# A seam between two phases laid out anew: one residual instruction, one square, h by pairs of feature tiles, weight splits behind them

## The chip, the core and the metric

The kernel runs on one core of one Trainium2 chip. The metric is the device time of one launch in microseconds. The core's engines are TensorE (PE, with the weight loads shown apart as PEld), VectorE (DVE), ScalarE (ACT), GpSimd (POOL) and SyncE (SP, which only issues DMAs here). Each runs its own instructions in order, and waits for the others by semaphores.

## What is computed

Two layers of a transformer block with three parts: half a feed-forward (ffn a), a token mixer, half a feed-forward (ffn b). They run on 256 latent tokens `x` and 256 context tokens `ctx`, 1024 features each, in float32:

```python
def _rmsnorm(x, g):
    return x * lax.rsqrt(jnp.mean(x * x, axis=-1, keepdims=True) + EPS) * g

def _half_ffn(x, mod, g_pre, g_post, wg, wu, wd):
    shift, scale, gate = mod
    h = _rmsnorm(x, g_pre) * (1 + scale) + shift
    y = (jax.nn.silu(h @ wg) * (h @ wu)) @ wd
    return x + 0.5 * gate * _rmsnorm(y, g_post)

# mixer: the same frame around m @ w_out, where m is the gated sum of
# a gated linear attention, a Fourier mix and a latent attention over w_in's outputs
# for each layer: ffn a on x and ctx, mixer on both, ffn b on both;
# the last layer's mixer output and ffn b are needed for x alone
```

So between two parts each token row is finished (`x + gate * rmsnorm(y)`), normed again, scaled and shifted by feature, and fed to the next part's first matrix products.

## The kernel before

**Layout.** The 512 tokens (context, then latent) are four *token tiles* of 128 rows: `x` is one SBUF tile [128, 4, 1024] with tokens on partitions. The input of each part, `h`, stands the other way, features on partitions: eight feature tiles [128, 512 tokens]. Every float32 product is made of three matmuls: each operand is split into a hi part (rounded to fp32r) and a lo part (the rest), and hi x hi, lo x hi and hi x lo are summed in PSUM (`acc`, L479 to L481; `mul`, L530 to L532).

**Phases.** There are six: ffn a, mixer, ffn b of each layer. A phase ends in `down`, which multiplies by `wd` (tile name d) or `wout` (o) with tokens on PSUM's partitions, in two column halves of 512. In the second half the last k-tiles, six in an ffn and eight in a mixer, are *held*: `seam` runs them token tile by token tile, so that tile 0 is finished while TensorE still works on tiles 1 to 3. That makes 18 or 24 matmuls a token tile.

**The seam.** In it TensorE, DVE, ACT and POOL keep the order in which the code is written (`manual_schedule`); outside of it a scheduler orders them. For each token tile: `evac` squares and sums the PSUM on ACT (sink<-d, L536) and multiplies it by the gate's row on DVE (dy, L537); `mean_eps` adds the two half sums and EPS on DVE (nv, L450); `root` is a power of -0.5 on POOL (nr, L455); `residual` adds to x in two halves of 512 on DVE (L465), each followed by a square and sum on ACT (sink<-x, L469); then another `mean_eps` and `root`, and `normed_x` makes n on DVE (L474). TensorE transposes n, eight times 128x128, into four PSUM banks pt, each of which holds two feature tiles of 256 tokens (L431). `pre_tile` scales and shifts each feature tile: ACT writes hi straight from PSUM (L440); for even tiles DVE computes the same value unrounded, pnt, from the same bank (L442) and subtracts hi (L443); for odd tiles ACT writes pnt (L445) and POOL subtracts (L446).

Tokens 0 to 255 (n0, n1) are the first half; the transposes of n0 stand after tile 2's held matmuls, those of n1 at two thirds of tile 3's, and their `pre_tile` calls are strewn between tile 3's steps. The second half (n2, n3) is a closure, `late`.

**The next phase** starts with `dense_pair`: three blocks in a mixer (zx, zk, zk; 144 matmuls of 256 columns) or four in an ffn (pg, pu, pg, pu; 192), first for tokens 0 to 255, then for 256 to 511. It calls `late` after the fifth of eight k-steps of the first half. In a mixer the result zx is copied by ACT (zxs, L657), and a chain over DVE, ACT and TensorE follows that ends in the decays; zq are the projections beside it.

**Weights** come as raw tiles of 512 KB through SP's DMA queue into four buffers. `Stream.pump` issues loads as buffers come free, and splits the weights (ACT CAST, L144; DVE subtraction, L145) 8 or 9 half-units ahead of their use. It is called whenever the next half-unit of weights is taken, so within `dense_pair` too.

**The seams** are counted in the text: 0 (ffn a to mixer, layer 0), 1 (mixer to ffn b), 2 (ffn b to ffn a of layer 1), 3 (ffn a to mixer) and 4 (mixer to ffn b, layer 1). Seams 0 to 3 have all four token tiles. Seam 4 has tiles 2 and 3 alone, without an early half, and so has the end, where the rows of x go out instead (four DMAs of 256 KB, L467).

## Time and profile before

| | us |
|---|---|
| median of 3 runs (lowest, highest) | 2222.96 (2221.34, 2223.61) |
| the profiled execution | 2223.26 |
| its span, first to last instruction | 2221.4 |
| TensorE busy | 2123.8 (96%) |
| DVE busy | 1323.6 (60%) |
| ACT busy | 880.2 (40%) |
| POOL busy | 198.5 (9%) |

The mean granted clock of TensorE is 0.986 of full speed. How to read it: an engine's busy share is an average over stages that have different limits. What a change in one stage is worth is read from that stage: where TensorE stood idle in it, for how long, and who released it. The views used below are the windows (busy time of each engine in a stretch), the timeline (instructions in order of time, with the idle time ahead of one in brackets and what ended it), the waits (who waited for whom) and the page's groups. Columns such as 128x512 are partitions by elements. Matmuls overlap, so one that is listed with 0.39 us may follow another after 0.23: paces are read from starts.

### The profile page before, as it was taken

What the parts mean: (1) busy time and instruction counts of PE and PEld (TensorE: products, weight loads), DVE (VectorE), ACT (ScalarE), POOL (GpSimd) and SP (SyncE); (2) the same over time, 40 slices, a digit from 0 to 9 for tenths busy, and PEclk for the clock granted to TensorE, in tenths of its full rate; (3) what the DMA queues carried; (4) which work ended last, traced back from release to release, by engine and by line L of the source; (5) the groups of instructions that cost most, each with busy time, mean ns of one, the idle gap of its engine ahead of it and who ended that gap; (6) DMA issues with size and microseconds to landing.
All of it is one profiled execution on the core that took longest, in us unless ns stands there. A gap on an engine that the chain in (4) does not pass through costs nothing.

```text
span 2221.4 us, 33022 instructions
## 1 busy us (share of the span) xinstructions
PE 2123.8 (96%) x12928; PEld 1791.3 (81%) x12928; DVE 1323.6 (60%) x2554; ACT 880.2 (40%) x1747; POOL 198.5 (9%) x220
## 2 busy tenths in 40 slices
PE   6999999899999999999999989999998999998998
PEld 5788888677777788888888868888887788997997
DVE  4877677567566634478776545333334677765554
ACT  4332223644344523443233344232225545545443
POOL 1000000134120100100000010000001232100000
PEclk9999999999999999999999999999999999998999
DMA  8555476131111223256557615232431323453553
GB/s 306 191 190 198 162 242 213 48 105 40 55 48 58 91 81 128 72 165 203 192 188 267 215 55 172 81 114 76 134 113 39 114 65 96 154 193 131 177 192 123
DMA packets 88436, 304.52 MB, mean 137 GB/s; under 512 B 10520, under 2 KB 13848, under 8 KB 88280
## 3 DMA queue, kind: packets, MB, share of 16 engines
q1 hardware_dynamic: 86328, 296.88, 39.9%
q10 hardware_dynamic: 1952, 5.53, 0.7%
q8 instruction: 101, 1.65, 0.3%
q14 instruction: 55, 0.45, 0.1%
HBM read 301.23 MB, written 1.15 MB: 136 GB/s over the span
## 4 chain that ended last, share of the span: by engine, by line
PE 80%; DVE 6%; ACT 5%; DMA 3%; issue 3%; POOL 2%; ACTq 0%; SPq 0%; POOLq 0%; DVEq 0%
PE d L531 6%; PE d L532 6%; PE d L530 6%; PE pu L481 6%; PE pg L481 6%; PE pu L480 6%; PE pu L479 6%; PE pg L479 5%; PE pg L480 5%; PE ga L481 3%; PE ga L479 3%; PE ga L480 3%; DMA raw<-wmod 2%; PE br L479 1%; PE br L481 1%
## 5 line engine op out<-in xcount | busy, mean ns | idle before, releaser
L145 DVE TENSOR_TENSOR w<-raw,w 128x512 fp32r<-128x512 f32 (+2 forms) x824 | 532.8, 691 | 155.1 <-ACT w L144 152.3
L144 ACT CAST w<-raw 128x512 fp32r<-128x512 f32 (+2 forms) x824 | 460.4, 612 | 298.5 <-DMA raw<-wd 82.2
L303 DVE SCALAR_TENSOR_TENSOR raw<-raw,cbc 128x1024 f32<-128x1024 f32 x128 | 156.5, 1223 | 36.0 <-DMA raw<-wmod 33.7
L303 DVE SCALAR_TENSOR_TENSOR junk<-raw,cbc 128x1024 f32<-128x1024 f32 x96 | 117.2, 1221 | 82.9 <-DMA raw<-wmod 82.8
L610 DVE TENSOR_TENSOR sg<-sg,pu 128x512 f32<-128x512 f32 (+1 forms) x88 | 54.3, 617 | 150.9 <-PE pu L481 136.9
L455 POOL TENSOR_TENSOR nr<-nv,cst 128x1 f32<-128x1 f32 x38 | 21.0, 552 | 1370.5 <-DVE nv L450 1370.5
L609 ACT ACTIVATE sg<-pg 128x512 f32<-128x512 f32 (+1 forms) x88 | 47.4, 540 | 78.5 <-PE pg L481 78.2
L481 PE MATMUL pg<-h10l,w 128*128 128x512 f32 (+1 forms) x192 | 72.0, 376 | 5.6 <-DVE h10l L443 4.2
L479 PE MATMUL ga<-h01h,w 128*128 128x512 f32 x192 | 76.0, 396 | 0.0
L481 PE MATMUL ga<-h01l,w 128*128 128x512 f32 x192 | 75.6, 394 | 0.0
L479 PE MATMUL pg<-h02h,w 128*128 128x512 f32 (+1 forms) x192 | 72.2, 376 | 3.3 <-ACT h02h L440 3.3
L481 PE MATMUL pg<-h02l,w 128*128 128x512 f32 (+1 forms) x192 | 72.5, 378 | 2.7 <-DVE h02l L443 1.5
L480 PE MATMUL ga<-h01h,w 128*128 128x512 f32 x192 | 74.9, 390 | 0.0
L537 DVE TENSOR_TENSOR dy<-d,gr 128x512 f32<-128x512 f32 x28 | 19.1, 690 | 93.0 <-ACT sink L536 92.7
L817 DVE SCALAR_TENSOR_TENSOR tg<-tg,br 128x512 f32<-128x512 f32 (+1 forms) x48 | 26.4, 551 | 77.6 <-PE br L481 68.5
L479 PE MATMUL pg<-h10h,w 128*128 128x512 f32 (+1 forms) x192 | 71.6, 373 | 1.1 <-ACT h10h L440 1.0
L479 PE MATMUL pu<-h10h,w 128*128 128x512 f32 (+1 forms) x192 | 71.5, 372 | 1.0 <-ACT w L144 1.0
L479 PE MATMUL pg<-h00h,w 128*128 128x512 f32 x176 | 69.0, 392 | 3.4 <-ACT h00h L440 3.4
L481 PE MATMUL pu<-h02l,w 128*128 128x512 f32 (+1 forms) x192 | 72.0, 375 | 0.0
L480 PE MATMUL pu<-h02h,w 128*128 128x512 f32 (+1 forms) x192 | 71.9, 375 | 0.0
L480 PE MATMUL pg<-h02h,w 128*128 128x512 f32 (+1 forms) x192 | 71.9, 374 | 0.0
L479 PE MATMUL pu<-h02h,w 128*128 128x512 f32 (+1 forms) x192 | 71.8, 374 | 0.0
(518 smaller groups left out, 5933.4 us busy)
## 6 DMA issues: line engine op xcount, KB each, us to landing
raw<-wgu SPq DMA_DIRECT2D x170, 512.0 KB, 4.3
raw<-wmod SPq DMA_DIRECT2D x128, 512.0 KB, 4.3
raw<-win SPq DMA_DIRECT2D x92, 512.0 KB, 3.4
raw<-wd SPq DMA_DIRECT2D x88, 512.0 KB, 4.2
raw<-wm SPq DMA_DIRECT2D x16, 512.0 KB, 7.8
raw<-wbr SPq DMA_DIRECT2D x16, 512.0 KB, 3.5
raw<-wout SPq DMA_DIRECT2D x16, 512.0 KB, 4.1
gr<-rows SPq DMA_DIRECT2D x10, 512.0 KB, 6.5
```

The costliest lines, as they stand in the source:

```text
L144: nc.scalar.copy(hi, w)
L145: nc.vector.tensor_tensor(lo, w, hi.bitcast(F32), ALU.subtract)
L303: nc.vector.scalar_tensor_tensor(w if r else self.junk, w, 1.0, self.cbc[r], ALU.mult, ALU.mult, accum_out=m[:, t, r:r + 1])
L479: nc.tensor.matmul(ps, lhsT=hi, rhs=rhi, start=first, stop=False)
L480: nc.tensor.matmul(ps, lhsT=lo, rhs=rhi, start=False, stop=False)
L481: nc.tensor.matmul(ps, lhsT=hi, rhs=rlo, start=False, stop=last)
L530: nc.tensor.matmul(ps, lhsT=hi, rhs=w[0], start=kt == 0, stop=False)
L531: nc.tensor.matmul(ps, lhsT=hi, rhs=w[1], start=False, stop=False)
L532: nc.tensor.matmul(ps, lhsT=lo, rhs=w[0], start=False, stop=kt == n - 1)
L609: nc.scalar.activation(sg[:, t0:512], pg[:, t0:512], AF.Silu)
L610: nc.vector.tensor_tensor(sg[:, t0:512], sg[:, t0:512], pu[:, t0:512], ALU.mult)
L817: nc.vector.scalar_tensor_tensor(x, x, 1.0, ps[:, t0:512], ALU.add, ALU.mult)
```

## The change

- `x` and `sink` get a 1025th column, which POOL sets once to (1024 x EPS)^0.5. The square of x over 1025 columns, scaled by 1/1024, then sums to mean + EPS, so that DVE's `mean_eps` for x goes.
- The residual is one DVE instruction of 1024 columns, the square one ACT instruction of 1025 (`squares`), with the root right behind it.
- The transposes of n0 stand in the middle of tile 2's held matmuls, those of n1 in the middle of tile 3's.
- `pre_tile` in the seams becomes `pre_pair`, for two feature tiles at a time: ACT writes both unrounded from the bank (pnt), DVE rounds them to hi in one cast of 2x256 columns and subtracts in another instruction. POOL and DVE no longer make pnt or lo from the bank; POOL keeps the roots alone. The h tiles, which hold two feature tiles each, have names by pair now (h010 is pair 0 of h01).
- `late` comes one k-step later, and within `dense_pair` the stream is `lazy`: it doesn't split weights ahead until `late` has been issued.
- `late` takes the transposes of n2 and n3 by turns, feature tile by feature tile. (The start of the program, which makes the first h, uses the same function for its transposes.)
- The output's rows go out in two DMAs of 512 KB.

```diff
@@ class Stream
+        self.lazy = False
@@ next
-            self.pump()
+            if not self.lazy or self.s not in self.parts:
+                self.pump()
@@ setup
-        self.x = c.tile([128, 4, D], F32, name="x")
-        self.sink = c.tile([128, D], F32, name="sink")
+        self.x = c.tile([128, 4, D + 1], F32, name="x")
+        self.sink = c.tile([128, D + 1], F32, name="sink")
+        nc.gpsimd.memset(self.x[:, :, D:D + 1], (D * EPS) ** 0.5)
...
+    def turned(self, out, ns):
+        for t in range(NT):
+            for j, n in ns:
+                self.nc.tensor.transpose(out[t // 2][:, t % 2, 128 * j:128 * j + 128], n[:, 128 * t:128 * t + 128], self.ident)
+        return out
+    def pre_pair(self, l, which, hf, u, bank):
+        nc = self.nc
+        sl = slice(256 * hf, 256 * hf + 256)
+        A, B = (self.modv[l][3 * which + a] for a in (1, 0))
+        tmp = self.s("pnt", (2, 256))
+        for w in range(2):
+            t = 2 * u + w
+            nc.scalar.activation(tmp[:, w, :], bank[:, w, :], AF.Identity, bias=B[:, t, hf:hf + 1], scale=A[:, t, hf:hf + 1])
+        def parts():
+            hi, lo = self.h2[0][u][:, :, sl], self.h2[1][u][:, :, sl]
+            nc.vector.tensor_copy(hi, tmp)
+            nc.vector.tensor_tensor(lo, tmp, hi.bitcast(F32), ALU.subtract)
+        return parts
...
-    def residual(self, j, r, out):
...
+    def residual(self, j, r):
+        xj = self.x[:, j, 0:D]
+        self.nc.vector.scalar_tensor_tensor(xj, self.y[j], r, xj, ALU.mult, ALU.add)
+    def squares(self, j):
+        sx = self.v("sx", 1)
+        self.nc.scalar.activation(self.sink, self.x[:, j, :], AF.Square, scale=D ** -0.5, accum_out=sx)
+        return self.root(sx)
@@ dense_pair
+        self.W.lazy = True
...
-                if hf == 0 and kt == NT - 4:
+                if hf == 0 and kt == NT - 3:
                     self.late()
+                    self.W.lazy = False
+                    self.W.pump()
@@ seam
         for j in tiles:
             for i, (kt, w) in enumerate(held):
-                if turned and j == last and i == 2 * len(held) // 3:
-                    self.turn_tile(turned, 1, ns[1])
+                if ahead and j >= last - 1 and i == len(held) // 2:
+                    t = j - last + 1
+                    self.turned(pts, [(t, ns[t])])
                 mul(ps[j], kt, w, j)
-            if turned and j == last:
-                half(0, turned, range(2))
+            if ahead and j == last:
+                pair()
+                parts[0]()
+            if nxt and j > first:
+                rx[j - 1] = self.squares(j - 1)
+            if ahead and j == last:
+                pair()
             evac(ps[j], j, 1)
-            if nxt and j > tiles[0]:
-                close(j - 1)
             r = self.root(self.mean_eps(ss[j][:, 0:1], ss[j][:, 1:2]))
-            if turned and j == last:
-                half(0, turned, range(2, 4))
-            sx[j] = self.residual(j, r, nxt is None)
-            if turned and j == last - 1:
-                self.turn_tile(turned, 0, ns[0])
+            if ahead and j == last:
+                parts[1]()
+                pair()
+            if nxt and j > first:
+                close(j - 1)
+            self.residual(j, r)
+            if not nxt:
+                self.nc.sync.dma_start(self.io["out"][j - 2], self.x[:, j, 0:D])
         if nxt:
-            if turned:
-                half(0, turned, range(4, 6))
+            if ahead:
+                parts[2]()
+                pair()
+            rx[last] = self.squares(last)
+            if ahead:
+                parts[3]()
             close(last)
-            if turned:
-                half(0, turned, range(6, NT))
-            self.late = lambda: half(1, self.turned([ns[2], ns[3]]))
+            def late():
+                for u, bank in enumerate(self.turned(self.banks(), [(0, ns[2]), (1, ns[3])])):
+                    self.pre_pair(*nxt, 1, u, bank)()
+            self.late = late
```

DVE in seam 0, from tile 0's residual to tile 1's; dy_2395 and dy_2396 are tiles 0 and 1 before, n_3231 is n0. Before:

```order
397 L465 SCALAR_TENSOR_TENSOR x<-dy_2395,nr,x 128x512 x2
398 L537 TENSOR_TENSOR dy_2396<-d,gr_2441 128x512
399 L450 SCALAR_TENSOR_TENSOR nv<-sx 128x1
400 L474 TENSOR_SCALAR n_3231<-x,nr 128x1024
401 L450 SCALAR_TENSOR_TENSOR nv<-ss_2400 128x1
402 L465 SCALAR_TENSOR_TENSOR x<-dy_2396,nr,x 128x512 x2
```

and now, with dy_2396 as tile 0 and n_3232 as n0:

```order
397 L482 SCALAR_TENSOR_TENSOR x<-dy_2396,nr,x 128x1024
398 L557 TENSOR_TENSOR dy_2397<-d,gr_2442 128x512
399 L472 SCALAR_TENSOR_TENSOR nv<-ss_2401 128x1
400 L491 TENSOR_SCALAR n_3232<-x,nr 128x1024
401 L482 SCALAR_TENSOR_TENSOR x<-dy_2397,nr,x 128x1024
```

Each tile has one row less: the small sum of the squares of x is gone. The instruction of n stands behind the next tile's evacuation and sum in both.

ACT in seam 0, at the second half: the last two of eight weight casts in a row (w) and the late h tiles behind them (h01h from PSUM, pnt unrounded). Before:

```order
253 L144 CAST w_3402<-raw_3375 128x512
254 L144 CAST w_3406<-raw_3375 128x512
255 L440 ACTIVATE h01h_3164<-pt,m_3_1214,m_4_1537 128x256
256 L445 ACTIVATE pnt<-pt,m_3_1214,m_4_1537 128x256
257 L440 ACTIVATE h01h_3165<-pt,m_3_1214,m_4_1537 128x256
258 L144 CAST w_3411<-raw_3389 128x512
259 L440 ACTIVATE h01h_3166<-pt,m_3_1214,m_4_1537 128x256
260 L440 ACTIVATE h01h_3165<-pt,m_3_1214,m_4_1537 128x256
261 L445 ACTIVATE pnt<-pt,m_3_1214,m_4_1537 128x256
```

and now, from tile 3's square (sink<-x) to the first two of nine casts:

```order
238 L486 ACTIVATE sink,sx<-x 128x1025
239 L684 DMA tabq<-tabq 128x1024
240 L447 ACTIVATE pnt<-pt,m_3_1215,m_4_1538 128x256 x8
241 L147 CAST w_3447<-raw_3439 128x512
242 L147 CAST w_3450<-raw_3439 128x512
```

Before, all but one of the second half's twelve instructions stood behind the eight casts, and a ninth cast among them. Now all eight of the second half stand ahead of the casts.

TensorE in seam 0, around the end of tile 2 and the start of tile 3 (a16 to a20 are the held k-tiles in turn). Before:

```order
1586 L531 MATMUL d<-w_3129,a20h_2310 128x512
1587 L532 MATMUL d<-w_3129,a20l_2311 128x512
1588 L431 MATMUL pt<-cst,n_3231 128x128 x8
1589 L530 MATMUL d<-w_3046,a16h_1982 128x512
1590 L531 MATMUL d<-w_3046,a16h_1982 128x512
1591 L532 MATMUL d<-w_3046,a16l_1983 128x512
```

and now, in the middle of tile 2:

```order
1600 L551 MATMUL d<-w_3089,a18h_2143 128x512
1601 L552 MATMUL d<-w_3089,a18l_2144 128x512
1602 L436 MATMUL pt<-cst,n_3232 128x128 x8
1603 L550 MATMUL d<-w_3092,a18h_2143 128x512
1604 L551 MATMUL d<-w_3092,a18h_2143 128x512
1605 L552 MATMUL d<-w_3092,a18l_2144 128x512
```

The transposes of n0 moved by nine matmuls towards the front.

## Rows read from the trace of the kernel before

**Rows 1.** Page part 4, the chain that ended last: share of the span by engine.

```profile
PE 80%; DVE 6%; ACT 5%; DMA 3%; issue 3%; POOL 2%; ACTq 0%; SPq 0%; POOLq 0%; DVEq 0%
```

**Rows 2.** Windows, five seams: stretch; length; busy PE, PEld, DVE, ACT, POOL (count); clock; DMA.

```profile
387.14:432.86 45.72, 37.71 (x232) 32.41 (x230) 25.80 (x50) 25.20 (x58) 11.01 (x16) 0.96 0.19 58
913.20:966.50 53.30, 47.24 (x297) 42.67 (x296) 24.20 (x48) 27.34 (x59) 10.72 (x16) 0.94 0.22 77
1291.64:1343.90 52.26, 42.60 (x279) 37.07 (x279) 30.89 (x59) 27.26 (x60) 11.18 (x16) 1.00 0.31 103
1669.00:1713.40 44.40, 37.16 (x238) 31.70 (x236) 24.65 (x48) 24.15 (x56) 10.94 (x16) 1.00 0.14 48
2005.00:2045.00 40.00, 31.39 (x193) 29.15 (x192) 21.58 (x40) 20.69 (x45) 5.18 (x8) 0.83 0.39 131
```

**Rows 3.** Timeline, TensorE, seam 0: start, us, work, [idle before <- releaser].

```profile
386.98 0.39 PE L530 MATMUL d<-w,a16h 128*128 128x512 f32 x1
...
395.15 1.03 PE L431 MATMUL pt<-cst,n 128*128 128x128 f32 x8
395.94 0.48 PE L530 MATMUL d<-w,a16h 128*128 128x512 f32 x1
...
400.50 1.09 PE L431 MATMUL pt<-cst,n 128*128 128x128 f32 x8 [1.58 <-DVE n L474]
...
422.40 0.38 PE L479 MATMUL zx<-h01h,w 128*128 128x256 f32 x1 [1.63 <-ACT h01h L440]
...
432.14 0.28 PE L480 MATMUL zk<-h01h,w 128*128 128x256 f32 x1
...
432.62 0.28 PE L481 MATMUL zk<-h01l,w 128*128 128x256 f32 x1
```

**Rows 4.** Waits of TensorE: waiter <- releaser, us in total, times, longest.

```profile
PE pt L431 <- DVE n L474: 11.5, 7, 3.1
PE zq L479 <- ACT kq L669: 9.6, 2, 4.9
...
PE pg L479 <- ACT h02h L440: 3.3, 1, 3.3
```

**Rows 5.** Timeline, seam 0: ACT, then DVE, then POOL.

```profile
404.54 0.56 ACT L440 ACTIVATE h01h<-pt,m,m 128x256 fp32r<-128x256 f32 x1 [0.61 <-DVE pnt L442]
...
417.62 4.26 ACT L144 CAST w<-raw 128x512 fp32r<-128x512 f32 x8
...
409.31 1.41 DVE L465 SCALAR_TENSOR_TENSOR x<-dy,nr,x 128x512 f32<-128x512 f32 x2
...
410.07 1.24 POOL L446 TENSOR_TENSOR h01l<-pnt,h01h 128x256 fp32r<-128x256 f32 x1 [0.90 <-ACT pnt L445]
```

**Rows 6.** Page part 5: weight subtraction, 1024-column multiply, root; busy and mean ns.

```profile
L145 DVE TENSOR_TENSOR w<-raw,w 128x512 fp32r<-128x512 f32 (+2 forms) x824 | 532.8, 691 | 155.1 <-ACT w L144 152.3
...
L303 DVE SCALAR_TENSOR_TENSOR raw<-raw,cbc 128x1024 f32<-128x1024 f32 x128 | 156.5, 1223 | 36.0 <-DMA raw<-wmod 33.7
...
L455 POOL TENSOR_TENSOR nr<-nv,cst 128x1 f32<-128x1 f32 x38 | 21.0, 552 | 1370.5 <-DVE nv L450 1370.5
```

**Rows 7.** One line or tile: ns min/median/max. Square, n and POOL's lo part.

```profile
L361 ACT ACTIVATE sink<-x x2: 1039/1048/1057, 5.4 to 8.7; 128x1024 f32<-128x1024 f32 x2
...
L474 DVE TENSOR_SCALAR n<-x,nr x4: 752/753/755, 393.7 to 415.0; 128x1024 f32<-128x1024 f32 x4
...
L446 POOL TENSOR_TENSOR h01l<-pnt,h01h x8: 728/736/1237, 405.6 to 427.8; 128x256 fp32r<-128x256 f32 x8
```

**Rows 8.** Timeline, TensorE, seam 4.

```profile
2020.25 1.97 PE L431 MATMUL pt<-cst,n 128*128 128x128 f32 x8 [2.67 <-DVE n L474]
...
2034.97 0.44 PE L479 MATMUL pu<-h12h,w 128*128 128x256 f32 x1 [2.89 <-ACT sg L609]
```

**Rows 9.** Page part 6, DMA issues: size and median us to landing.

```profile
raw<-win SPq DMA_DIRECT2D x92, 512.0 KB, 3.4
```

**Rows 10.** Line 467, the output's four DMAs of 256 KB.

```profile
DMA to landing us min/median/max: 2.0/2.0/2.0
```

More of the change, by code (lines that the diff above doesn't have):

```diff
@@ L419, in new_h, with banks @@
     def new_h(self, name):
[L420 to L431 removed]
+        self.h2 = [[self.c([2, 512], f"{name}{j}{w}", F32R) for j in range(NT // 2)] for w in "hl"]
+        self.hi, self.lo = ([h[t // 2][:, t % 2, :] for t in range(NT)] for h in self.h2)
+    def banks(self):
+        return [self.aux("pt", (2, 256)) for _ in range(4)]
+    def turned(self, out, ns):
+        for t in range(NT):
+            for j, n in ns:
+                self.nc.tensor.transpose(out[t // 2][:, t % 2, 128 * j:128 * j + 128], n[:, 128 * t:128 * t + 128], self.ident)
+        return out
+    def pre_pair(self, l, which, hf, u, bank):
[11 more added lines that the diff above has]
+        return parts
     def pre_tile(self, l, which, hf, t, n):
@@ L456, in root @@
         return r
-    def residual(self, j, r, out):
-        nc = self.nc
-        sx = self.v("sx", 2)
-        for h in range(2):
-            sl = slice(512 * h, 512 * h + 512)
-            xj = self.x[:, j, sl]
-            nc.vector.scalar_tensor_tensor(xj, self.y[j][:, sl], r, xj, ALU.mult, ALU.add)
-            if out:
-                nc.sync.dma_start(self.io["out"][j - 2][:, sl], xj)
-            else:
-                nc.scalar.activation(self.sink[:, sl], xj, AF.Square, scale=D ** -0.5, accum_out=sx[:, h:h + 1])
-        return sx
+    def residual(self, j, r):
+        xj = self.x[:, j, 0:D]
+        self.nc.vector.scalar_tensor_tensor(xj, self.y[j], r, xj, ALU.mult, ALU.add)
[3 more added lines that the diff above has]
+        return self.root(sx)
     def normed_x(self, j, r):
         n = self.c([D], f"n{j}")
-        self.nc.vector.tensor_scalar(n, self.x[:, j, :], r, None, ALU.mult)
+        self.nc.vector.tensor_scalar(n, self.x[:, j, 0:D], r, None, ALU.mult)
         return n
@@ L563, in seam @@
     def seam(self, tiles, held, ps, mul, evac, ss, nxt):
-        full, last = len(tiles) == 4, tiles[-1]
-        ns, sx = {}, {}
-        turned = [self.aux("pt", (2, 256)) for _ in range(4)] if full and nxt else None
-        def half(hf, banks, ts=range(NT)):
-            for t in ts:
-                self.pre_tile(*nxt, hf, t, banks[t // 2][:, t % 2, :])
+        full, first, last = len(tiles) == 4, tiles[0], tiles[-1]
+        ns, rx = {}, {}
+        ahead = full and nxt
+        pts = self.banks() if ahead else None
@@ L575, in close, with pair @@
+        parts = []
+        def pair():
+            u = len(parts)
+            parts.append(self.pre_pair(*nxt, 0, u, pts[u]))
         def close(j):
-            ns[j] = self.normed_x(j, self.root(self.mean_eps(sx[j][:, 0:1], sx[j][:, 1:2])))
+            ns[j] = self.normed_x(j, rx[j])
         for j in tiles:
             for i, (kt, w) in enumerate(held):
-                if turned and j == last and i == 2 * len(held) // 3:
-                    self.turn_tile(turned, 1, ns[1])
+                if ahead and j >= last - 1 and i == len(held) // 2:
+                    t = j - last + 1
+                    self.turned(pts, [(t, ns[t])])
```

23 lines of the change are left out of this document (8 added, 15 removed).

## The prediction

> **What bounds the kernel now.** I read the page's chain first: TensorE carries 80% of the chain that ended last [rows 1], so time is won only where TensorE stands still or runs slowly. Next I listed TensorE's idle time in order of time. It is bunched in the four full "seams", where one phase hands over to the next: three tiles of held matmuls, 32 transposes, then the first projections in two halves. Each has a row in [rows 2], from the end of tile 0's last held matmul to the last matmul of the projections: 45.72, 53.30, 52.26 and 44.40 us for seams 0 to 3.
>
> What would these stretches take if TensorE never waited? [Rows 3] has the paces: the 36 matmuls of tiles 1 and 2 go from 386.98 to 395.15, so 0.227 each and 4.08 us a tile; eight transposes take 0.79 (395.15 to 395.94); a 256-column matmul takes 0.12 (four in 0.48, 432.14 to 432.62). Seams 0 and 3 are three tiles (12.2), 32 transposes (3.2) and 144 projection matmuls (17.3): 32.7. Seam 2 has 192 matmuls: 38.4. Seam 1 has 24 matmuls a tile (5.45) and 192: 42.5. So 13.0, 10.8, 13.9 and 11.7 us, **49.4 in all, are waiting, or a slow pace after a wait**. That is what the change can win there.
>
> Of what the waits consist is seen in seam 0. TensorE stands 1.58 before the transposes of n1, whose DVE instruction isn't done, and 1.63 before an h tile of the second half (400.50 and 422.40) [rows 3]; over the run the transposes wait 11.5 us for n [rows 4]. The h tiles are late for two reasons [rows 5]: ACT's h waits 0.61 for DVE's pnt, which reads the same PSUM bank, in turn and not beside it; and at 417.62 eight weight casts, 4.26 us, stand on ACT ahead of nearly all of the second half's h tiles.
>
> **The change part by part.** I walk through seam 0 in us after 387.14, with hops of 0.04 to 0.08 between engines.
>
> *Residual and squares.* Two halves take 1.41 on DVE [rows 5]; one 128x1024 instruction of the same kind 1.22 [rows 6], saving 0.2. One Square of 128x1024 takes 1.05 [rows 7], and 0.1 more to its sum; but it can't start until the whole residual is done, where the first half's square ran beside the second half's residual. Dropping the small DVE sum (EPS now comes in as a column) saves 0.2. So the chain per tile is about as long as before: tile 0's residual 2.18 to 3.40, square to 4.65, root (0.55 on POOL [rows 6]) to 5.25. On DVE the next tile's evacuation and sum stand ahead; n0 (0.75 [rows 7]) ends at 6.8.
>
> *Transposes moved.* n0 now stands in the middle of tile 2, at 6.1: wait 0.75. n1 is ready at 11.95 where TensorE wants it at 11.8: wait 0.25. Before, the second waited 1.58. Tile 3 ends at 14.9.
>
> *Pairs instead of tiles.* ACT alone now reads the bank (two instructions of 0.56 [rows 5]), DVE makes the hi part with a new 128x512 cast, and the lo part by a subtraction, 0.69 at most, what the weight's subtraction of that size takes [rows 6]. The cast is not in the trace. Its bounds: half of n's 0.75 [rows 7], thus 0.38, and the two-input subtraction's 0.69. I take the middle, 0.55: n has one input in SBUF as the cast has, but another output type. The walk was made with 0.45; the 0.1 is added below. Pair 0 is complete at 14.75, before tile 3 ends; pairs 1 and 2 cost waits of 0.3 and 0.2; pair 3 (22) is in time. POOL's lo parts, of which one took 1.24 beside a DVE residual [rows 5], are gone.
>
> *Splits behind.* The late transposes follow n3 (22.5) and the eight late ACT instructions run at once, so the second half starts at 25.8 without a wait, where before it waited 1.63. The nine weight casts end at about 31.6, 3 us earlier in time than before's eight, and are covered by the second half's matmuls to 34.4. Without that cover they would hold the copy of zx, and with it the decay chain that ends in zq's wait of 4.8 us in each mixer [rows 4], which remains; for that I add 0 to 1, taken 0.5, a mixer.
>
> Waits left: 1.5, and 0.8 for slow first matmuls behind them: seam 0 takes 35.0 instead of 45.7, **-10.7**; seam 3, the same program, **-9.4**. In seam 1 the tiles are longer, so no transposes wait, and of the 3.3 us that the second half stood there for an h tile [rows 4] I keep 0.9: a table load and two Silus still come ahead of late pair work, the casts no longer. With 0.7 for slow firsts 44.1, **-9.2**. In seam 2 weights are still cast ahead of and between the late pairs: the 1.5 of seam 0, then 0.5, 1.7 and 0.8, and 0.7 for slow firsts, 43.6, **-8.7**.
>
> *Seam 4* works with two tiles and has no second half. Its last transposes stood 2.67 for n, and a later block 2.89 for ACT's sg [rows 8], at a granted clock of 0.83 [rows 2], so partly at the lower of the two levels. The h tiles come some 5 us earlier by pairs, but now the transposes of n2 stand between those of n3, so they can't go early: **-3** (-1.5 to -4.5).
>
> *Ends.* The output goes in 512 KB pieces: the last 256 KB landed in 2.0 [rows 10], a 512 KB load of the quick kind takes 3.4 [rows 9]; less 0.2 for the shorter residual: **+0.6** (0.3 to 1.2, since the first piece no longer goes out ahead). Setting the EPS column (one POOL instruction at the start) and the longer rows of x cost nothing: the loads of x hide them; uncovered, 0.5.
>
> Sum: -10.7 -9.2 -8.7 -9.4 -3 +0.6 = -40.4; +1.0 for the zx chain, +1.6 for the cast, 0.1 for each of four on the path of four seams: **-37.8**. From the profiled execution's 2223.26 (span 2221.4, 1.9 around it; 0.3 above the median of the runs) that is **2185.5**.
>
> One row bears on POOL's root. The lo part of 1.24 on POOL started at 410.07, while DVE's residual of 409.31 ran [rows 5]; the median of these is 0.74 [rows 7]. In the new order the roots of tiles 2 and 3 fall beside casts and subtractions on DVE. The Trainium skill (Advanced Engine Details and Errata, VectorE Performance Modes) says that the second Vector port is shared with GpSimd and that GpSimd instructions and two-port Vector instructions block each other. The long row fits a shared port, though the Vector instruction beside it has two tensor inputs; by the rule one root a seam would wait some 0.7 longer, an estimate, and the time would be 2.8 higher, 2188. I leave it out of the sum, since n2 and n3 are needed last.
>
> **The rivals.** *Half of it comes.* The chain per tile is no shorter, and now two transposes per seam are placed tightly inside the tiles. If the chain is 2 us longer than walked (the cast at 0.69, the roots held, ACT's squares in front of the evacuations), both positions wait, each 2 us, and the pairs behind the residual of tile 3 too: 5 us a seam back, 4 x 5 = 20: 2205. For it: ACT and DVE now have the lo parts that POOL had. Against: DVE's work in seam 0 sums to about 20 of 35 us.
>
> *Slower: the weights starve.* The four raw weight buffers aren't emptied until late, so no load goes out during most of a seam. If the fifth and later loads come too late, TensorE waits on weights after each seam. It decides when the loads behind the seam are later than the nine splits cover: 4.5 blocks of 24 matmuls, 24.5 us. Price: 12 us a seam where it fails, 4 x 12 = 48 less the 38 won, +10: 2233. Against: 512 KB of the mixer's land in 3.4 [rows 9], and the casts are, in time, no later than before.
>
> *It doesn't do what it says.* The seams get shorter, but the phase behind starts with the same waits, longer: zq's chain and the weights take the gain back, at 2215 to 2224, say 2220. Against: the zx copy moves with the seam.
>
> **How the numbers follow.** Forecast 0.68 (2172 to 2196, from the bounds of the cast, seam 4 and the ends, and walked waits halved or doubled), half 0.20, no gain 0.06, slower 0.06. The range leaves out the last two and a tail: 2172 to 2208. This kernel's measurement tells 0.2% (4.4 us) from no change: faster 0.89, same 0.05, slower 0.06.
>
> **What would show it.** Right: the seams' stretches 35, 44, 44 and 35 us; no wait of ACT for DVE's reading of a bank; transposes waiting under 1.2 us in a seam; the eight late ACT instructions ahead of the casts, and no wait over 1 us at the second half outside of seam 2; the cast at 0.38 to 0.69. Wrong: waits of the transposes over 2 us, TensorE waiting on weights within 25 us behind a seam, a longer wait of zq, or a granted clock below 0.95 in seam 2 or 3, where it was 1.00 [rows 2].

## The result

The changed kernel takes 2183.64 us (median of four, 2180.90 to 2184.99) against 2223.28 for the kernel before. The ratio is 0.9819, with a 95% interval of 0.9807 to 0.9831: 39.6 us or 1.8% faster. The prediction was 2185.5, in a range of 2172 to 2208. The profiled execution took 2184.58, its span 2182.8, which is 38.6 less than before's 2221.4. One execution of before_lazy, a kernel of the experiments, took 11842.65 us and is left out of its median below.

The page of the changed kernel: TensorE's busy time and the chain, which answers to [rows 1], and POOL's root, which answers to the root of [rows 6].

```profile
PE 2110.0 (97%) x12928; PEld 1782.3 (82%) x12928; DVE 1318.3 (60%) x2516; ACT 856.7 (39%) x1675; POOL 171.9 (8%) x185
...
PE 69%; DVE 13%; DMA 8%; ACT 5%; issue 4%; POOL 2%; ACTq 0%; POOLq 0%; DVEq 0%
...
L477 POOL TENSOR_TENSOR nr<-nv,cst 128x1 f32<-128x1 f32 x20 | 14.8, 741 | 1374.4 <-DVE nv L472 1374.4
```

TensorE is busy for 13.8 us less, though it does the same matmuls: matmuls that wait or run slowly count as busy too (in seam 0, 232 records with 37.71 before [rows 2], 231 with 34.20 now). The chain is no guide to this: it goes through DMA and DVE for a larger part now (8% and 13%, before 3% and 6%), though TensorE waits less. The last row is a surprise that comes back below: roots behind an evacuation take 0.74 on average, where all took 0.55 before.

The same five windows as in [rows 2], cut by the same events:

```profile
388.17:423.72 35.55, 34.20 (x231) 30.59 (x229) 24.49 (x42) 20.13 (x42) 5.27 (x8) 1.00 0.16 49
903.50:947.50 44.00, 43.30 (x298) 40.12 (x298) 23.68 (x40) 22.20 (x43) 5.29 (x8) 1.00 0.29 95
1274.36:1318.65 44.29, 40.57 (x280) 36.67 (x279) 28.65 (x49) 21.73 (x44) 5.21 (x8) 1.00 0.36 118
1643.75:1679.38 35.63, 34.22 (x232) 30.63 (x230) 23.20 (x40) 18.99 (x40) 5.21 (x8) 1.00 0.15 47
1970.00:2010.00 40.00, 33.98 (x232) 31.86 (x231) 25.03 (x44) 22.20 (x47) 2.66 (x4) 0.91 0.39 132
```

| stretch, us (a sign marks a difference to before) | before | predicted | after |
|---|---|---|---|
| start to seam 0 | 387.14 | 387.14 | 388.17 |
| seam 0 | 45.72 | 35.0 | 35.55 |
| seam 1 | 53.30 | 44.1 | 44.00 |
| seam 2 | 52.26 | 43.6 | 44.29 |
| seam 3 | 44.40 | 35.0 | 35.63 |
| between seams 0 and 1, 1 and 2, 2 and 3 | 1130.6 | +0.5 | +1.2 |
| from seam 3 to tile 3's evacuation in seam 4 | 299.3 | +0.5 | +0.1 |
| from there to the last evacuations | 198.0 | -3 | -5.2 |
| the end | 10.8 | +0.6 | +0.5 |

(The prediction's 1.6 for a dearer cast stands in no row of its own; its 1.0 for the zx chain stands in the two rows of +0.5.) So the four full seams give 36.2 of the 38.6 us, and each took what the walk through it had given, within 0.7. The granted clock is 1.00 in all of them, where it was 0.96 and 0.94 in seams 0 and 1; only seam 4, with 0.91 for 0.83, still has a part at the lower level. A part of the gain is that clock. Before, TensorE stood 1.63 and then 0.93 at the second half of seam 0, and the 256-column matmuls behind these waits followed each other after 0.21 (424.23 to 427.22), where 0.12 is the pace elsewhere:

```profile
422.00:427.00 5.00, 3.68 (x17) 3.47 (x18) 4.87 (x10) 4.79 (x11) 2.12 (x3) 0.71 0.96 298
```

The granted clock of this stretch was 0.71, so partly the lower of the two levels, and 14 matmuls lost 1.3 us. In the changed kernel no part of the seam runs so.

Seam 0 on TensorE, all its waits, which answers to [rows 3]:

```profile
395.12 1.09 PE L436 MATMUL pt<-cst,n 128*128 128x128 f32 x8 [0.83 <-DVE n L491]
...
400.58 1.09 PE L436 MATMUL pt<-cst,n 128*128 128x128 f32 x8 [0.26 <-DVE n L491]
...
406.16 0.39 PE L496 MATMUL zx<-h011h,w 128*128 128x256 f32 x1 [0.27 <-DVE h011h L451]
```

The walk had said 0.75, 0.25, 0.3 and a fourth wait of 0.2, which isn't there. There is no wait in the second half, where 1.63 stood before. In all, eleven waits took 7.9 us of this seam before, and three take 1.4 now. The waits of TensorE over the whole run, as in [rows 4]:

```profile
PE zq L496 <- ACT kq L704: 9.7, 2, 4.9
PE pt L436 <- DVE n L491: 9.4, 8, 3.7
...
PE pg L496 <- DVE h100h L451: 1.4, 1, 1.4
...
PE pg L496 <- DVE h020h L451: 0.7, 1, 0.7
```

The wait of 3.3 for h02h has become 0.7; zq still waits for kq as long as before, as the prediction had it; and 1.4 before the second half of seam 2 is left, where six weight casts, and two Silus that wait 2.6 for their load, stand on ACT ahead of the late pairs (1296.18 to 1303.90). ACT in seam 0 shows why the second half doesn't wait, and DVE's row gives the cast that the trace of before could not show:

```profile
412.27 3.76 ACT L447 ACTIVATE pnt<-pt,m,m 128x256 f32<-128x256 f32 x8 [2.25 <-PE pt L436]
415.88 4.29 ACT L147 CAST w<-raw 128x512 fp32r<-128x512 f32 x8
421.91 0.62 ACT L147 CAST w<-raw 128x512 fp32r<-128x512 f32 x1 [1.74 <-DMA raw<-win]
...
L451 DVE CAST h010h<-pnt x2: 421/424/427, 402.2 to 413.3; 128x512 fp32r<-128x512 f32 x2
```

The eight late pnt come as soon as their transposes are done; the eight casts follow them, 1.7 us earlier in time than before [rows 5], and the ninth waited for its load and ends 0.6 before zx is done. The cast takes 0.42, within the bounds of 0.38 and 0.69, and below the 0.55 taken.

### The profile page after: what moved, and what is told of

It is laid out like the page before. It is cut to its first block, busy times and chain, and to the rows that moved or that the text cites. A ratio compares the mean times of both kernels' runs of the same rounds, so it can differ in the third digit from the quotient of the medians.

```text
span 2182.8 us, 32890 instructions
## 1 busy us (share of the span) xinstructions
PE 2110.0 (97%) x12928; PEld 1782.3 (82%) x12928; DVE 1318.3 (60%) x2516; ACT 856.7 (39%) x1675; POOL 171.9 (8%) x185
## 4 chain that ended last, share of the span: by engine, by line
PE 69%; DVE 13%; DMA 8%; ACT 5%; issue 4%; POOL 2%; ACTq 0%; POOLq 0%; DVEq 0%
DMA raw<-wmod 6%; PE d L551 6%; PE d L552 6%; PE d L550 6%; PE pg L498 3%; PE pu L498 3%; PE pg L496 3%; PE pu L496 3%; PE pu L497 3%; PE pg L497 3%; PE ga L498 3%; PE ga L496 3%; PE ga L497 3%; DVE junk L309 3%; DVE raw L309 2%
## 5 line engine op out<-in xcount | busy, mean ns | idle before, releaser
L309 DVE SCALAR_TENSOR_TENSOR raw<-raw,cbc 128x1024 f32<-128x1024 f32 x128 | 156.4, 1222 | 38.2 <-DMA raw<-wmod 35.9
L309 DVE SCALAR_TENSOR_TENSOR junk<-raw,cbc 128x1024 f32<-128x1024 f32 x96 | 117.3, 1221 | 86.1 <-DMA raw<-wmod 85.9
L842 ACT ACTIVATE tg<-ga 128x512 f32<-128x512 f32 (+1 forms) x48 | 23.6, 491 | 64.0 <-PE ga L498 63.9
L1121 ACT ACTIVATE pr<-sc,nb 128x512 f32<-128x512 f32 (+1 forms) x48 | 29.6, 617 | 43.1 <-DVE nb L1118 38.9
L447 ACT ACTIVATE pnt<-pt,m,m 128x256 f32<-128x256 f32 x72 | 34.8, 569 | 18.4 <-PE pt L436 18.4
L550 PE MATMUL o<-w,mh 128*128 128x512 f32 x96 | 37.5, 391 | 0.0
L552 PE MATMUL o<-w,ml 128*128 128x512 f32 x96 | 37.4, 389 | 0.0
L551 PE MATMUL o<-w,mh 128*128 128x512 f32 x96 | 37.4, 389 | 0.0
L981 POOL TENSOR_TENSOR f<-f,kq 128x512 f32<-128x512 f32 (+1 forms) x24 | 34.2, 1436 | 32.0 <-ACT f L979 31.9
L436 PE MATMUL pt<-cst,n 128*128 128x128 f32 x176 | 26.1, 298 | 10.2 <-DVE n L491 9.4
L1117 DVE TENSOR_REDUCE mx<-sc 128x1 f32<-128x512 f32 (+1 forms) x48 | 28.3, 590 | 9.2 <-PE sc L498 9.0
L864 POOL TENSOR_TENSOR mp<-tg 128x512 f32<-128x512 f32 (+1 forms) x16 | 20.0, 1253 | 172.6 <-DVE tg L852 149.0
L436 PEld LDWEIGHTS pt<-cst,n 128*128 128x128 f32 x176 | 21.7, 154 | 14.2 <-DVE n L491 12.6
```

Of the source, the lines that this page charges most:

```text
L309: nc.vector.scalar_tensor_tensor(w if r else self.junk, w, 1.0, self.cbc[r], ALU.mult, ALU.mult, accum_out=m[:, t, r:r + 1])
L436: self.nc.tensor.transpose(out[t // 2][:, t % 2, 128 * j:128 * j + 128], n[:, 128 * t:128 * t + 128], self.ident)
L550: nc.tensor.matmul(ps, lhsT=hi, rhs=w[0], start=kt == 0, stop=False)
L551: nc.tensor.matmul(ps, lhsT=hi, rhs=w[1], start=False, stop=False)
L552: nc.tensor.matmul(ps, lhsT=lo, rhs=w[0], start=False, stop=kt == n - 1)
```

## The experiments

Four take one part out of the changed kernel. The edits are small; where a part is undone, the order of the rest stays the new one.

**Splits not behind.**

```diff
@@ dense_pair
-        self.W.lazy = True
```

> The changed kernel with one line less: the stream splits weights ahead within the pair of projections again, so in seams 0 and 3 eight casts (about 4.3 us on ACT, 5 us of subtractions on DVE) stand ahead of the second half's h. My theory (the splits behind are a part of the gain): the second half waits some 3 us in seams 0 and 3, 1 to 2 us in seams 1 and 2, in sum 7 to 12 us: 2191 to 2196 us. Rival (the order of the splits is worth nothing, since the weights are needed soon after and the same work must be done): 2180 to 2187 us, with a shorter wait of zq or of a weight to make up for it.

2190.48 us (ratio to before 0.9839, 0.9823 to 0.9855): 6.8 slower than the changed kernel by the medians, 4.4 by the ratios, whose intervals overlap. TensorE in seam 0, ACT ahead of it, and the seam's stretch:

```profile
418.96 0.39 PE L496 MATMUL zx<-h010h,w 128*128 128x256 f32 x1 [1.72 <-DVE h010h L451]
...
412.04 4.26 ACT L147 CAST w<-raw 128x512 fp32r<-128x512 f32 x8
416.20 1.46 ACT L447 ACTIVATE pnt<-pt,m,m 128x256 f32<-128x256 f32 x3
...
390.29:427.81 37.52, 34.45 (x231) 30.64 (x230) 24.23 (x42) 20.04 (x42) 5.27 (x8) 1.00 0.22 71
```

Eight casts, 4.26 us, stand ahead of the late pnt again, and the second half waits 1.72. Seam 0 takes 37.5 for 35.6 and seam 3 37.0 for 35.6; seams 1 and 2 lie within 0.7 of the changed kernel's. Of the 7.0 between the two profiled executions, 2.1 lie ahead of seam 0, where up to 384 us both run the same instructions in the same order. So the splits behind are worth 4 to 7 us, less than I had expected. The rival, that their order is worth nothing, falls by seams 0 and 3, and zq's wait, 9.7 in two, is no shorter.

**No pairs.**

```diff
@@ pre_pair
...
-            nc.scalar.activation(tmp[:, w, :], bank[:, w, :], AF.Identity, bias=B[:, t, hf:hf + 1], scale=A[:, t, hf:hf + 1])
+            nc.scalar.activation(hi[w], bank[:, w, :], AF.Identity, bias=sc[w][1], scale=sc[w][0])
+        nc.scalar.activation(tmp[1], bank[:, 1, :], AF.Identity, bias=sc[1][1], scale=sc[1][0])
@@ parts
-            nc.vector.tensor_copy(hi, tmp)
-            nc.vector.tensor_tensor(lo, tmp, hi.bitcast(F32), ALU.subtract)
+            nc.vector.tensor_scalar(tmp[0], bank[:, 0, :], sc[0][0], sc[0][1], ALU.mult, ALU.add)
+            nc.vector.tensor_tensor(lo[0], tmp[0], hi[0].bitcast(F32), ALU.subtract)
+            nc.gpsimd.tensor_tensor(lo[1], tmp[1], hi[1].bitcast(F32), ALU.subtract)
```

> The changed kernel with the scale and shift by single feature tiles as before (ACT writes hi from PSUM, DVE makes pnt of the even tile from the same bank, POOL subtracts for the odd one), in the new order. My theory (ACT and DVE reading one bank in turn, and POOL's slow subtraction, made h late): 2 to 3 us in each of four full seams and 2 in seam 4, 2193 to 2198 us. Rival (the pairs move work without freeing the path, since DVE now has the hi casts): within 4 us of the changed kernel, 2180 to 2187 us.

2192.50 us (0.9857, 0.9842 to 0.9872): 8.9 slower. TensorE in seam 0, and one of POOL's lo parts, which it has again:

```profile
407.13 0.39 PE L501 MATMUL zx<-h011l,w 128*128 128x256 f32 x1 [0.66 <-DVE h011l L454]
...
410.40 0.33 PE L436 MATMUL pt<-cst,n 128*128 128x128 f32 x1 [0.54 <-DVE pnt L453]
...
407.63 1.19 POOL L455 TENSOR_TENSOR h012l<-pnt,h012h 128x256 fp32r<-128x256 f32 x1
```

TensorE waits for DVE's lo part and for its reading of the bank (0.66, 0.54), and POOL's subtractions take up to 1.19. The four full seams are 1.7, 0.8, 2.8 and 1.7 longer. The pairs are worth 9 us where the rest is in place, a little under my range; the rival falls.

**The transposes back.** n0 behind tile 2, n1 at two thirds of tile 3.

```diff
@@ seam
-                if ahead and j >= last - 1 and i == len(held) // 2:
-                    t = j - last + 1
-                    self.turned(pts, [(t, ns[t])])
+                if ahead and j == last and i == 2 * len(held) // 3:
+                    self.turned(pts, [(1, ns[1])])
...
             self.residual(j, r)
+            if ahead and j == last - 1:
+                self.turned(pts, [(0, ns[0])])
```

> The changed kernel with the transposes of n0 back behind tile 2 and those of n1 back at two thirds of tile 3. My theory: the waits of 0.83 and 0.26 us for n0 and n1 in each seam behind an ffn vanish, but the first pair of h is ready 0.5 to 1 us after tile 3 is done, and TensorE waits there: within 3 us of the changed kernel, 2181 to 2187 us. Rival (the place of the transposes is a main part of the gain, as they start the h work earlier): 2 us a seam more, 2190 us or above.

2183.08 us (0.9810, 0.9795 to 0.9824), the same as the changed kernel. Its only two waits in seam 0:

```profile
400.40 1.09 PE L436 MATMUL pt<-cst,n 128*128 128x128 f32 x8 [0.33 <-DVE n L491]
...
405.98 0.39 PE L496 MATMUL zx<-h011h,w 128*128 128x256 f32 x1 [0.55 <-DVE h011h L451]
```

The wait of 0.83 for n0 is gone, and the one before the second pair has grown from 0.27 to 0.55. The place of the transposes is worth nothing where the rest is in place.

**The residual in halves**, two squares and the small sum on DVE, with the sum and the root still ahead of the next evacuation.

```diff
@@ residual
...
-        self.nc.vector.scalar_tensor_tensor(xj, self.y[j], r, xj, ALU.mult, ALU.add)
+        for h in range(2):
+            sl = slice(512 * h, 512 * h + 512)
+            xj = self.x[:, j, sl]
+            self.nc.vector.scalar_tensor_tensor(xj, self.y[j][:, sl], r, xj, ALU.mult, ALU.add)
@@ squares
...
+        for h in range(2):
+            sl = slice(512 * h, 512 * h + 512)
+            self.nc.scalar.activation(self.sink[:, sl], self.x[:, j, sl], AF.Square, scale=D ** -0.5, accum_out=sx[:, h:h + 1])
-        return self.root(sx)
+        return self.root(self.mean_eps(sx[:, 0:1], sx[:, 1:2]))
```

> The changed kernel with the residual in two halves of 512, two squares and the small sum with EPS on DVE, in the new order. My theory: the chain per tile gets 0.2 to 0.5 us longer, which is paid where n0 and n1 are waited for, in three seams, and twice in seam 4: 1 to 4 us, 2185 to 2188 us. Rival (the instruction count on DVE and ACT is what the gain comes from): 2190 us or above.

2183.71 us (0.9813, 0.9798 to 0.9827): the same, and under the 2185 to 2188 that I had expected. The one instruction and the column of EPS, which give the change its name, win nothing by themselves.

These four sum to 15 of the 40 us. So I asked whether pairs and splits relieve the same place, or something else carries the rest. Four more kernels make the table of both parts, in the old order and in the new one (the edits are those above, and for the old order the same lines of the change put into the kernel before):

> The changed kernel without the lazy splits and without the pairs: what is left of the change is the order of the code in the seam, the placed transposes and the single residual and square. Each part taken away alone cost 6.8 and 8.9 us of the 40. Theory A (the two relieve the same place, the second half's h, so that either alone wins most of it): over 2204 us, more than the sum of the two. Theory B (they add up, and the order of the seam makes the other 24 us): 2197 to 2201 us.

> The kernel before with the lazy splits alone (and the second half issued one step later, as in the change). Theory A: -10 to -15 us, 2208 to 2213 us, since the second half's h no longer stands behind eight casts. Theory B (the parts add up): about -7 us, 2216 us.

> The kernel before with h made by pairs in the seams (two ACT instructions, one cast and one subtraction on DVE), in the old order. Theory A: -12 to -20 us, 2203 to 2211 us, since POOL's subtractions and the waits for one bank go in both halves. Theory B: about -9 us, 2214 us.

> The kernel before with both, so that of the change only the order in the seam, the placed transposes and the single residual and square are missing. Theory A: -30 us or more, 2193 us or less, the order being worth under 10 us. Theory B: 2205 to 2209 us, the order being worth over 20 us.

| median, us | old order | new order | the order is worth |
|---|---|---|---|
| neither | 2223.6 (before) | 2197.50 (undo_both) | 26 |
| splits behind | 2213.08 (before_lazy) | 2192.50 (undo_pairs) | 21 |
| pairs | 2209.78 (before_pairs) | 2190.48 (undo_lazy) | 19 |
| both | 2199.35 (before_lazy_pairs) | 2183.64 (changed) | 16 |

(Ratios to before: undo_both 0.9879, 0.9864 to 0.9895; before_lazy 0.9952, 0.9935 to 0.9968; before_pairs 0.9942, 0.9925 to 0.9958; before_lazy_pairs 0.9891, 0.9876 to 0.9906.) Neither theory fits all four: undo_both lies where B has it, before_pairs in A's range, and the other two lie between. In the old order the two parts add up (10.5 and 13.9 alone, 24.3 together). In the new one each is worth 5 to 7 us less (5.0 and 7.0 alone), and the 13.9 of both together is their sum within the spread of undo_both's four runs (2193.29 to 2199.36). So they don't stand for each other, and the order of the seam is the largest part. What in it? Not the places of the transposes. Two candidates were left: the order of n and the roots, and the places of the pairs among tile 3's steps.

**n behind its root.** The kernel with the residual in halves, and with before's order of a tile's small steps on DVE and POOL.

```diff
@@ squares
-        return self.root(self.mean_eps(sx[:, 0:1], sx[:, 1:2]))
+        return sx
@@ seam
             evac(ps[j], j, 1)
+            if nxt and j > first:
+                close(j - 1)
             r = self.root(self.mean_eps(ss[j][:, 0:1], ss[j][:, 1:2]))
...
-            if nxt and j > first:
-                close(j - 1)
             self.residual(j, r)
@@ close
-            ns[j] = self.normed_x(j, rx[j])
+            ns[j] = self.normed_x(j, self.root(self.mean_eps(rx[j][:, 0:1], rx[j][:, 1:2])))
```

> The changed kernel with the old order of the small steps of a token tile on DVE and POOL: the sum of the squares of x behind the next tile's evacuation, its root, n, and only then the sum and the root of the evacuation and the next residual (with the residual and the square in halves, which alone cost nothing). In the changed order the root of the evacuation runs while DVE makes n. My theory (this order is the main part of the 16 to 26 us that pairs and splits don't explain): each tile's chain gets 0.9 to 1.5 us longer, and n1 and the pairs behind it are late by that in four seams, seam 4 too: 8 to 14 us, 2191 to 2198 us. Rival (the order of n and the roots is hidden, and the gain comes from where the pairs stand among tile 3's steps): within 4 us, 2180 to 2187 us.

2193.24 us (0.9869, 0.9856 to 0.9883): 9.6 slower, as expected; the four full seams are 2.9, 2.2, 2.5 and 2.9 longer. TensorE in seam 0, and DVE from tile 1's evacuation to its residual:

```profile
394.64 1.09 PE L436 MATMUL pt<-cst,n 128*128 128x128 f32 x8 [1.28 <-DVE n L495]
...
400.93 1.09 PE L436 MATMUL pt<-cst,n 128*128 128x128 f32 x8 [1.07 <-DVE n L495]
...
407.81 0.64 PE L436 MATMUL pt<-cst,n 128*128 128x128 f32 x4 [1.36 <-DVE nv L472]
...
392.41 0.69 DVE L561 TENSOR_TENSOR dy<-d,gr 128x512 f32<-128x512 f32 x1 [1.57 <-ACT sink L560]
393.02 0.15 DVE L472 SCALAR_TENSOR_TENSOR nv<-sx 128x1 f32<-128x1 f32 x1
393.83 0.75 DVE L495 TENSOR_SCALAR n<-x,nr 128x1024 f32<-128x1024 f32 x1 [0.66 <-POOL nr L477]
394.50 0.15 DVE L472 SCALAR_TENSOR_TENSOR nv<-ss 128x1 f32<-128x1 f32 x1
395.32 1.42 DVE L484 SCALAR_TENSOR_TENSOR x<-dy,nr,x 128x512 f32<-128x512 f32 x2 [0.66 <-POOL nr L477]
```

DVE waits twice for POOL here, 0.66 for n's root and 0.66 for the residual's, one after the other, so the residual starts 2.9 us after the evacuation. In the changed kernel the second root runs while DVE makes n, and it starts 1.9 after (393.64 to 395.51, below). TensorE pays with 1.28 and 1.07 for the early transposes, and 1.36 and 0.38 for the late ones, instead of 0.83, 0.26 and none. The kernel undoes the place of x's sum and root and the place of n together, so which of the two weighs more was not tried. This is the part that the edit of the residual and squares was in truth for: the root of x is out of the way before the evacuation comes.

**With the transposes back too**, by the edit shown above.

> The kernel of n_behind_root (2193.2 us) with the transposes of n0 and n1 back in their old places too. It then differs from before_lazy_pairs (2199.4 us) mainly by where the pairs and the squares stand among tile 3's steps. If the transposes' new places are worth something as long as n is late: 2196 to 2199 us. If they are a loss there (n0 is waited for in the middle of tile 2), and the rest is the places of pairs and squares: 2190 to 2194 us.

2192.93 us (0.9858, 0.9841 to 0.9874), in the second of the two ranges: the transposes are worth nothing here either. What now differs from before_lazy_pairs, 6.4 us, is mainly the places of pairs and squares on ACT among tile 3's steps. TensorE and ACT of before_lazy_pairs around the first pair:

```profile
405.33 0.39 PE L497 MATMUL zx<-h010h,w 128*128 128x256 f32 x1 [1.90 <-DVE h010h L437]
...
402.46 0.63 ACT L487 ACTIVATE sink<-x 128x512 f32<-128x512 f32 x1 [3.85 <-DVE x L483]
...
403.82 1.00 ACT L435 ACTIVATE pnt<-pt,m,m 128x256 f32<-128x256 f32 x2
```

and ACT and TensorE of n_root_turn there:

```profile
402.55 1.02 ACT L447 ACTIVATE pnt<-pt,m,m 128x256 f32<-128x256 f32 x2 [2.80 <-PE pt L436]
403.60 0.64 ACT L490 ACTIVATE sink<-x 128x512 f32<-128x512 f32 x1
...
405.42 0.39 PE L502 MATMUL zx<-h010l,w 128*128 128x256 f32 x1 [0.29 <-DVE h010l L452]
```

In the old order the first pair's pnt stands behind the two squares of tile 2, which wait for the residual, and TensorE waits 1.90 for the pair. In the new one the code puts pnt ahead of the squares, and the wait is 0.29; the transposes of n1 start 13.35 after the start of the seam in both. Yet n_root_turn then waits 1.37 and 0.39 for the late transposes, where before_lazy_pairs waits 0.46, so the waits of the seam sum to 3.6 and 3.9. Its stretch is 38.1 for 39.6 all the same: behind the 1.90 the granted clock of before_lazy_pairs was 0.66 from 405 to 410, and matmuls of 256 columns followed after 0.21; n_root_turn has 1.00 there, and 0.12. That ACT's order is a cause is seen; that it makes up all of the 6.4 us is not shown, since the order of the late transposes and the output's DMAs differ as well.

**n ahead of the evacuation.** In the changed kernel a root on POOL is slow where DVE makes n beside it. DVE, then POOL, of the changed kernel in seam 0:

```profile
393.64 0.69 DVE L557 TENSOR_TENSOR dy<-d,gr 128x512 f32<-128x512 f32 x1 [2.00 <-ACT sink L556]
...
394.32 0.75 DVE L491 TENSOR_SCALAR n<-x,nr 128x1024 f32<-128x1024 f32 x1
395.51 1.29 DVE L482 SCALAR_TENSOR_TENSOR x<-dy,nr,x 128x1024 f32<-128x1024 f32 x1 [0.44 <-POOL nr L477]
...
392.97 0.55 POOL L477 TENSOR_TENSOR nr<-sx,cst 128x1 f32<-128x1 f32 x1 [2.65 <-ACT sink L486]
394.48 0.99 POOL L477 TENSOR_TENSOR nr<-nv,cst 128x1 f32<-128x1 f32 x1 [0.96 <-DVE nv L472]
```

The first root (0.55) runs while DVE stands; the second starts 0.16 after n, takes 0.99, and ends 0.40 after n does. DVE then stands 0.44 for it. `n_early` moves `close(j - 1)` ahead of `evac(ps[j], j, 1)`, nothing else.

> The changed kernel with n of a tile made ahead of the next tile's evacuation on DVE and not behind it. In the trace of the changed kernel the root on POOL takes 0.93 to 0.99 us where it runs beside DVE's n, and 0.55 elsewhere, and DVE stands 0.44 us for it each time. My theory (n holds POOL's root up): every root takes 0.55 to 0.60, the 0.44 us idle of DVE go, and the transposes of n0 stand under 0.2 us instead of 0.83: 2 to 4 us in all, 2179 to 2182 us. Rival (the root is slow for another reason): the roots stay at 0.9 us, and the evacuation is later by n's 0.7: 2184 to 2188 us.

2182.65 us (0.9818, 0.9805 to 0.9832), not to be told from the changed kernel. POOL's roots (min, median, max of all 20 behind an evacuation), DVE, and the only wait left in seam 0's first half:

```profile
L477 POOL TENSOR_TENSOR nr<-nv,cst x20: 548/548/598, 389.4 to 2175.3; 128x1 f32<-128x1 f32 x20
...
393.19 0.75 DVE L491 TENSOR_SCALAR n<-x,nr 128x1024 f32<-128x1024 f32 x1 [1.91 <-POOL nr L477]
393.86 0.68 DVE L557 TENSOR_TENSOR dy<-d,gr 128x512 f32<-128x512 f32 x1
...
405.81 0.39 PE L496 MATMUL zx<-h011h,w 128*128 128x256 f32 x1 [0.55 <-DVE h011h L451]
```

The mechanism is right: no root takes over 0.60. The transposes no longer wait either, but that is because n itself stands ahead of the evacuation. The size was wrong: with them in time, the next wait (the second pair's hi, 0.27 before) grew to 0.55, and since n holds the evacuation up now, tile 2's residual starts 12.80 after the start of the seam in both kernels. So what the slow root alone costs is not shown by this kernel.

**A faster version** has that, the cbc rows of the modulation (a table load and two Silus) behind the pair of projections, the late transposes of n2 ahead of those of n3, and four output DMAs of 256 KB again (shown are the late transposes and the cbc rows):

```diff
@@ late
-                for u, bank in enumerate(self.turned(self.banks(), [(0, ns[2]), (1, ns[3])])):
+                banks = self.banks()
+                for jn in ((0, ns[2]), (1, ns[3])):
+                    self.turned(banks, [jn])
+                for u, bank in enumerate(banks):
@@ ffn
-            if self.mods:
-                self.cond_rows()
             ps = []
...
+            if self.mods:
+                self.cond_rows()
```

> A try at a faster version: n ahead of the evacuation, the late transposes of n2 all ahead of those of n3, the condition rows of the modulation (a table load and two Silus on ACT) behind the pair of projections instead of ahead of the late pairs, and the last rows of x in four output DMAs of 256 KB. My theory: 2 to 4 us from n, 1 to 2 us from seams 1 and 2 (waits of 0.70, and of 1.39 and 0.53 us behind ACT), 0.4 in seam 4, 0.3 at the end: 2176 to 2180 us. Rival: the condition rows are needed early, and the multiplications with the modulation's weights, which start later, make the weights behind them late: 2182 us or above.

2177.92 us (0.9797, 0.9784 to 0.9811): 5.7 less than the changed kernel, and the fastest of all. Seam 2 is where most of it is, 41.3 for 44.3, which is 3.0 of the 4.5 between the two profiled executions:

```profile
1272.28:1313.59 41.31, 40.20 (x280) 36.48 (x279) 27.76 (x47) 21.96 (x44) 4.43 (x8) 1.00 0.29 95
```

The waits of 1.39 and 0.53 in its second half are gone. ACT comes to the late pairs without the Silus now, but what each of the small edits gives alone was not tried.

## Why the prediction was right, point by point

**What bounds the kernel.** Right: the time lay in TensorE's waits and slow paces in the seams, and counting the paces without waits gave what could be won. One row was cut wrongly: seam 3's stretch ran to 1713.40, but the last matmul of the pair of projections ends at 1712.46; six matmuls of zq stand behind it. So 0.9 of the -9.4 was never in that seam; by the right ends it won 7.8, and the four seams 35.3.

**Residual and squares.** The term (0.2 saved, the chain about as long) was right in sum and the reason was incomplete: the residual takes 1.29 and not 1.22, and undone alone it is worth nothing. What counts is that the root of x no longer stands behind the next evacuation, and that the evacuation's root runs beside n: n_behind_root puts 9.6 us on it. My walk had it in its times, since it followed the new order step by step, but the text named the wrong edits as the source, and the order, which is the largest part, has no term of its own in the sum.

**Transposes moved.** The waits were sized well (0.83 and 0.26 for 0.75 and 0.25), but the step "before, the second waited 1.58" credits the move with a gain it doesn't have: n1 came earlier, and undo_turn is as fast.

**Pairs and splits.** Right in direction: 8.9, and 4 to 7 us, by the kernels without them. The 1.6 us added for a dearer cast wasn't there (0.42 for a walk with 0.45), nor the 1.0 for the zx chain: the ninth cast waited 1.74 for its load and ended at 422.5, 2.8 later in the seam than walked, but the copy started only at 423.1.

**POOL's root.** I had looked for it in the wrong place. Beside the casts behind tile 3 a root takes 0.60; beside n, which the prediction doesn't name, two a seam take 0.93 to 0.99. The Trainium skill (Advanced Engine Details and Errata, VectorE Performance Modes) says that GpSimd instructions and two-port Vector instructions block each other, since the second Vector port is shared. The trace agrees as far as it goes: the root that starts 0.16 into n ends 0.40 behind it, and in n_early, with n out of the way, none takes over 0.60; which mode n runs in no run shows. It holds a residual up by 0.4 us, but no measured time hangs on it. The walk had n1 at 11.95, and it came at 12.36, but not for this. POOL, then DVE, of the changed kernel:

```profile
398.12 0.55 POOL L477 TENSOR_TENSOR nr<-sx,cst 128x1 f32<-128x1 f32 x1 [2.65 <-ACT sink L486]
...
399.10 0.69 DVE L557 TENSOR_TENSOR dy<-d,gr 128x512 f32<-128x512 f32 x1 [2.31 <-ACT sink L556]
...
399.78 0.75 DVE L491 TENSOR_SCALAR n<-x,nr 128x1024 f32<-128x1024 f32 x1
```

The root of n1 was done at 398.67, 1.1 before n1 started: n1 stood behind tile 2's evacuation, and that waited for tile 2's matmuls, which the wait for n0 (0.83 for 0.75) and a slow pace behind the transposes had made later.

**Seam 4** was mis-sized: -3 (-1.5 to -4.5), measured -5.2. Its transposes stand 2.29 and 3.73 now, answering to [rows 8]:

```profile
1980.95 0.66 PE L436 MATMUL pt<-cst,n 128*128 128x128 f32 x4 [2.29 <-DVE n L491]
1985.34 2.82 PE L436 MATMUL pt<-cst,n 128*128 128x128 f32 x12 [3.73 <-DVE n L491]
```

Before, they stood 3.06 (the 3.1 of [rows 4]) and 2.67. But the wait of 2.89 for sg has gone altogether, which the term did not count in full. So the waits sum to 6.0 for 8.6, which is 2.6 of the 5.2. The rest goes with the granted clock (0.91 for 0.83): before, the matmuls behind the wait for sg followed after 0.21 (2035.64 to 2038.41) at a clock of 0.66 between 2035 and 2040; now it is 1.00 from 1990 on. The term named the lower level and gave it no size.

**The end** was right in size: the two DMAs land in 2.6, between the rows of [rows 9] and [rows 10].

```profile
out<-x SPq DMA_DIRECT2D x2, 512.0 KB, 2.6
```

**What I had not seen.** The start came 1.0 us later, and between seams 1 and 2 the changed kernel takes 1.7 more. Neither can be put down to the change: in the nine other kernels with the new order seam 0 begins at 386.4 to 390.3 us, and the stretch between seams 1 and 2 takes 325 to 327. In the changed kernel TensorE loses 1.6 us there (at 1078 to 1134 us), at matmuls whose weight's lo part comes late from DVE. At the longest, 1123.14, DVE and ACT come late to the weight because DVE's multiplications for the modulation (L309) stand ahead, and one of them waits 3.25 for its own load (1118.00). So this is not the rival of the starving weights. That one fell: within 25 us behind a full seam TensorE waits for no weight. These two stretches (2.7) and the two terms that weren't there (2.6) cancel, as do seam 4 (2.2 more than forecast) and the full seams (36.2 for 38.0). That the sum is better than its terms is luck; that each seam came within 0.7 of its walk is not. The rival of half the gain fell, since the chain was not 2 us but 0.4 longer than walked at n1, though DVE's work in seam 0 came to 24.5 us and not to about 20; that the change doesn't do what it says fell with zq's unchanged wait.

## What to carry to other kernels

Where one engine has to be kept busy across a seam, write down each tile's chain on the helping engines and look for places where two short waits on a third engine stand one after the other: having the one root done before the next tile's work arrives, and running the other beside n, was worth 10 us here, merging the residual and the squares nothing. Work that nobody waits for yet, such as weights split ahead, belongs behind the work that releases the bound engine. Take the parts out one by one and in pairs before you believe which edit made the gain: the ones that look like the change may be worth nothing. And compare the stretches as well as the totals: of one difference of 7.0 us, 2.1 lay where both kernels run the same instructions.

## What the runs showed of the hardware

- A root of 128x1 on POOL takes 0.55, and 0.93 to 0.99 when DVE's n (128x1024, one SBUF input, 0.75) runs beside it; n itself isn't slowed. With n ahead of it all 20 take 0.55 to 0.60.
- DVE's cast from float32 to fp32r of 128x512 takes 0.42, its subtraction of that size 0.69.
- DVE's residual of 128x1024 takes 1.28 on average, on rows of x that are 1025 words apart; the multiply of the same operation on rows of 1024 takes 1.22 [rows 6]. The distance is hardly the reason: the residual in halves takes 0.75 each on rows of 1024 (before) and of 1025 (undo_residual). The two also differ in their scalar and in that the multiply sums; which of these it is wasn't tried.
- In three places a stretch of 5 us behind a wait of TensorE (1.63 with 0.93 in seam 0 before, 1.90 in before_lazy_pairs, 2.89 in seam 4 before) had a granted clock of 0.66 to 0.71, and matmuls of 256 columns followed after 0.21 for 0.12. Not every such wait did that: behind the 1.72 of undo_lazy's seam 0 the clock stayed at 1.00.
